# Down projections of a two-layer decoder trunk: unit by unit, in a pinned order of ScalarE and VectorE, with low parts on VectorE; two-bank attention scores; another end of the last norm

## The chip, the cores and the metric

The kernel runs on one core of a Trainium2 chip. The metric is the time of one execution in device microseconds; before the change the median of three runs is 2391.7 us (2388.97 to 2393.98). Lower is better.

## The reference

One sequence of 1024 tokens with 1024 channels passes two layers and a last RMSNorm, all in float32. Layer 0 mixes with retention heads and RWKV-7 heads, layer 1 with sliding-window attention (window 128, 16 query heads on 4 key heads, learned sinks). A SwiGLU feed-forward of width 2816 follows each. The change concerns the second product of the feed-forward, the scores of the attention and the last norm:

```python
def swiglu(h, w_gate, w_up, w_down):
    return (jax.nn.silu(h @ w_gate) * (h @ w_up)) @ w_down

s = jnp.einsum('bnqhgd,bnkhd->bnhgqk', q, kb).astype(jnp.float32) * HEAD_DIM ** -0.5   # then a band mask
h = h + mix
n = rms_norm(h, norm2_g[layer])
h = h + swiglu(n, ffn_w_gate[layer], ffn_w_up[layer], ffn_w_down[layer])
...
return rms_norm(h, final_g)
```

## The kernel before

**Layout.** Activations lie transposed: channels on the 128 partitions, tokens along the free axis, in two halves of 512 tokens. `h[0]` and `h[1]` hold the residual of the halves as 8 tiles of 128x512 each.

**Precision.** Every large product is split: an operand is rounded to the type fp32r (the high part, a ScalarE copy: `CAST` in the profile) and the rest is kept (the low part, a subtraction). A product then is three matmuls per 128x128 weight tile: high by high, high by low, low by high (`prod` L1174, `gemm` L346 to L348). A 128x512 matmul of this kind is the unit of PE's work. `vsplit` (L1345) splits weights of the down projection: high part on ScalarE (L1350), low part on GpSimd (L1351). `split` (L350) splits activations; the low part goes to GpSimd or to VectorE (L354), in the down projection half to each.

**Feed-forward.** The hidden width of 2816 is 22 tiles, taken as 11 pairs. Gate and up products follow a seven-product scheme in the manner of Strassen and Winograd: two products early (`ffn_early`) and five late (`late`, in five steps, for gate and up in lockstep with `form_down`, which prepares sums of hidden tiles for the down projection). `ffn_late` runs the eleven pairs. Hidden tiles go to the arrays `hid` in memory, their sums, split already, to `hc`.

**Down projection** (`down`, L1380). It also uses seven products in place of eight, over blocks of two output tiles, pairs of hidden tiles and the two token halves. The pairs are cut in groups: layer 0 has groups of 4 and 4 pairs (the other three pairs go through a plain product, `rest_d`), layer 1 has 4, 4 and 3. In a group there are seven stages, one per product, and in each stage four units, one for each block of output tiles (`dp`). A unit is 4 x 3 matmuls (3 x 3 in the group of three pairs) into one PSUM bank. Stage by stage:

- X, the moving operand, is either a plain hidden tile (loaded from `hid`, then split) or a prepared sum (loaded from `hc`, no split).
- Weights are loaded raw (`wdown`, 512 KB per load), combined on VectorE (`ws`, `wd`: three sums per block in the first stage, one in the third) and split before each unit.
- After a unit its bank is read: one or two VectorE adds into `h` or a helper (`vop`, L1377), or a ScalarE copy (L1411).

Four banks (tags f, f, f, y) serve stages 0 and 2, four others (m, m, r, c) stages 1, 3 and 4, the first four again stages 5 and 6 and then the next group.

**Order.** Each engine works in order. The order of the instructions on an engine is made at build time by a scheduler that follows the program's order and its own estimates of readiness; `keep` (L481) holds marked instructions in program order. SP issues nearly all DMAs. Tiles are taken from pools; a new pool on the place of a closed one waits for the last use of what lay there. PSUM has eight banks: the pool `ps` gives f three, m two, and r, c and y one each.

**Attention** (`attn`, L1498). For each of the two token halves, 4 key heads and 4 blocks of 128 queries: scores of 4 query heads (L1552, 64 rows of the array each, so e = 0 uses one half of the rows and e = 1 the other), into bank r for e = 0 and bank c for e = 1; one VectorE add of the mask per bank (L1556); maximum (L1562), exponentials, transposes, the product with V. Scores of e = 0 come first in the program, then those of e = 1.

**The last norm.** `final_r` (L1614) squares each tile on ScalarE (L1623), scales it by the gain on ScalarE (L1624), adds up squares on VectorE (L1626), sums over partitions with fp32 matmuls against a constant (L1629), and takes Ln and Exp (L1631, L1632), each with a load of its function table. For half 0 this runs beside the last two stages of the down projection; for half 1 after it. `final_out` multiplies (L1639: half 0 on GpSimd, half 1 on VectorE and GpSimd) and stores (L1640).

## Time and profile before

| | |
|---|---|
| median of three runs | 2391.7 us (2388.97, 2391.7, 2393.98) |
| profiled execution | 2394.0 us |
| its span, first to last instruction | 2392.2 us |
| mean granted clock of TensorE | 0.992 |
| down projection of layer 0 (seven products) | from 1149.5 us |
| attention, scores | 1386 to 1500 us, 1585 to 1701 us |
| down projection of layer 1 | 2151 to 2374 us |
| after its last product | 2374 to 2392 us |

Times within the execution count from the start of the span. In the views below, PE is TensorE's matmul, PEld its weight load, DVE VectorE, ACT ScalarE, POOL GpSimd and SP SyncE. A matmul's own row is longer than the distance to the next one, since they are pipelined: how much work a stretch did is read from the count of matmuls. A windows row gives the stretch, its length, then for each engine the busy time and, in brackets, the number of instructions, then the granted clock, the DMA share and GB/s. A waits row reads "who waited <- for whom: total, times, longest". A row of a line's or group's view gives minimum/median/maximum in ns, or busy us and mean ns; a timeline row gives start, duration, and in brackets the idle time before it and what ended it.

### The profile page before, as it was taken

To read this page: it belongs to the slowest core of one execution; us is meant where nothing else is said; L and a number is where in the kernel's file an instruction comes from. 1 tells how busy PE (TensorE), PEld (TensorE's weight loads), DVE (VectorE), ACT (ScalarE), POOL (GpSimd) and SP (SyncE) were. 2 spreads that over 40 slices of the span, in tenths; PEclk is the share of its full clock that TensorE was granted. 3 is DMA by queue.
4 is the path that set the end of the run, shared out by engine and by line. 5 is a ranking of instruction groups with operands and counts; after the bars stand their busy time and mean duration, and the time that the engine had idled before them with its cause. 6 is when DMAs were issued, how large, how long until landed. Compare 5 with 4: busy or idle time off the path is not lost. (4 is left out here: it accounts for less than half of the span.)

```text
span 2392.2 us, 35667 instructions
## 1 busy us (share of the span) xinstructions
PE 2318.9 (97%) x13098; PEld 1828.7 (76%) x13098; DVE 1626.3 (68%) x2462; ACT 1025.5 (43%) x1890; POOL 1193.1 (50%) x975
## 2 busy tenths in 40 slices
PE   8999899999999999999999999999999999999997
PEld 6776677777777888888778877677788788887785
DVE  5865855765567368885775469458638778887776
ACT  5354443324456333333333555455645233333336
POOL 7555331211541057776676632342232677767666
PEclk9999999999999999999999999999999999999999
DMA  7655454443445556563564321231336466547652
GB/s 267 197 204 188 154 165 133 126 128 115 146 172 181 198 171 212 195 216 137 217 222 153 118 62 58 66 131 62 106 128 220 159 217 218 203 178 274 219 200 107
DMA packets 167742, 395.93 MB, mean 166 GB/s; under 512 B 42896, under 2 KB 45584, under 8 KB 167568
## 3 DMA queue, kind: packets, MB, share of 16 engines
q1 hardware_dynamic: 164448, 388.15, 47.8%
q10 hardware_dynamic: 2832, 4.45, 0.6%
q8 instruction: 104, 1.70, 0.3%
q0 software_dynamic: 288, 1.05, 0.1%
q14 instruction: 70, 0.57, 0.1%
HBM read 271.29 MB, written 116.92 MB: 162 GB/s over the span
## 5 line engine op out<-in xcount | busy, mean ns | idle before, releaser
L332 POOL TENSOR_TENSOR w<-wr,w 128x512 fp32r<-128x512 f32 x196 | 264.3, 1354 | 427.9 <-ACT w L331 369.9
L239 PE MATMUL ps_f<-n,w 128*128 128x512 f32 x1440 | 383.5, 414 | 12.0 <-ACT w L331 6.4
L239 PEld LDWEIGHTS ps_f<-n,w 128*128 128x128 f32 x1440 | 268.3, 192 | 93.3 <-issue 21.9
L331 ACT CAST w<-wr 128x512 fp32r<-128x512 f32 x244 | 147.9, 612 | 188.8 <-PE ps_f L348 76.9
L332 POOL TENSOR_TENSOR w<-wq,w 128x512 fp32r<-128x512 f32 x92 | 130.5, 1430 | 31.7 <-ACT w L331 27.4
L346 PE MATMUL ps_f<-n,w 128*128 128x512 f32 x356 | 140.8, 396 | 2.6 <-ACT n L352 1.6
L347 PE MATMUL ps_f<-n,w 128*128 128x512 f32 x356 | 142.6, 400 | 0.0
L348 PE MATMUL ps_f<-n,w 128*128 128x512 f32 x356 | 140.1, 394 | 0.0
L1177 PE MATMUL ps_f<-n,w 128*128 128x512 f32 x322 | 127.5, 397 | 4.1 <-DVE h L1377 1.8
L1184 DVE TENSOR_TENSOR nq<-ps_m,u 128x512 f32<-128x512 f32 x88 | 58.7, 684 | 106.7 <-PE ps_m L1179 106.7
L1178 PE MATMUL ps_f<-n,w 128*128 128x512 f32 x322 | 125.5, 390 | 0.0
L1179 PE MATMUL ps_f<-n,w 128*128 128x512 f32 x322 | 125.2, 390 | 0.0
L354 POOL TENSOR_TENSOR n<-nq,n 128x512 fp32r<-128x512 f32 x64 | 106.0, 1667 | 10.2 <-ACT n L352 10.2
L1177 PE MATMUL ps_m<-n,w 128*128 128x512 f32 x282 | 110.6, 393 | 0.0
L1179 PE MATMUL ps_m<-n,w 128*128 128x512 f32 x282 | 109.8, 389 | 0.0
L1178 PE MATMUL ps_m<-n,w 128*128 128x512 f32 x282 | 109.8, 389 | 0.0
L332 POOL TENSOR_TENSOR wx<-wr,wx 128x512 fp32r<-128x512 f32 (+1 forms) x38 | 49.4, 1301 | 105.5 <-ACT wx L331 105.5
L1177 PE MATMUL ps_m<-cb,w 128*128 128x512 f32 x240 | 93.5, 389 | 0.9 <-DVE nq L1184 0.9
L1178 PE MATMUL ps_m<-cb,w 128*128 128x512 f32 x240 | 93.4, 389 | 0.0
L1179 PE MATMUL ps_m<-cb,w 128*128 128x512 f32 x240 | 93.4, 389 | 0.0
L1351 POOL TENSOR_TENSOR w<-wd,w 128x512 fp32r<-128x512 f32 (+1 forms) x53 | 75.9, 1442 | 32.0 <-ACT w L1350 31.8
L346 PEld LDWEIGHTS ps_f<-n,w 128*128 128x128 f32 x356 | 66.9, 188 | 20.0 <-ACT n L1598 2.2
(520 smaller groups left out, 6447.6 us busy)
## 6 DMA issues: line engine op xcount, KB each, us to landing
hc<-n SPq DMA_DIRECT2D x74, 512.0 KB, 2.7
wsp<-w SPq DMA_DIRECT2D x54, 512.0 KB, 3.4
w<-wsp SPq DMA_DIRECT2D x54, 512.0 KB, 3.7
wq<-in_w_gate SPq DMA_DIRECT2D x44, 512.0 KB, 4.2
u<-u SPq DMA_DIRECT2D x88, 256.0 KB, 2.9
n<-hc SPq DMA_DIRECT2D x43, 512.0 KB, 5.1
wr<-in_w_in SPq DMA_DIRECT2D x34, 512.0 KB, 5.0
hid<-n SPq DMA_DIRECT2D x66, 256.0 KB, 2.0
```

Of the source, the lines that this page charges most:

```text
L239: i = self.nc.tensor.matmul(out, lhsT, rhs, **kw)
L331: nc.scalar.copy(hi[:, :n], raw[:, c])
L332: self.lo.tensor_tensor(out=lo[:, :n], in0=raw[:, c], in1=hi.bitcast(F32)[:, :n], op=ALU.subtract)
L346: nc.tensor.matmul(ps, hi, rh, start=k == 0, stop=False)
L347: nc.tensor.matmul(ps, hi, rl, start=False, stop=False)
L348: nc.tensor.matmul(ps, lo, rh, start=False, stop=k == n - 1)
L354: e.tensor_tensor(out=lo, in0=src, in1=hi.bitcast(F32), op=ALU.subtract)
L1177: mm(ps, hi, xh, start=first and k == 0, stop=False, skip_group_check=True)
L1178: mm(ps, hi, xl, start=False, stop=False, skip_group_check=True)
L1179: mm(ps, lo, xh, start=False, stop=last and k == len(w) - 1, skip_group_check=True)
L1184: add = lambda o, x, y: V.tensor_tensor(out=o, in0=x, in1=y, op=ALU.add)
L1351: nc.gpsimd.tensor_tensor(out=lo, in0=v, in1=hi.bitcast(F32), op=ALU.subtract)
```

## The change

- `down` is written anew as a list of units. In each, in program order: the reads of the bank of the unit before (`post`); the weight split of the unit two ahead; the X split for the next stage; weight sums; loads of X two stages ahead and of the next group's weights (in stages 3 and 5); then the unit's matmuls. All ScalarE and VectorE instructions of it are chained by `pin`: each depends, for the order alone, on the one before on its engine.
- In `down` all low parts, of weights and of plain X, are on VectorE.
- For layer 0 the pool `fa` is opened, and the first weights, X and first weight split are done, before the last of the five late steps of the last feed-forward pair; a second pool `fw` (second halves of weights, sums) is opened after it. For layer 1 the first weight block is loaded into a raw tile of the feed-forward during the last pair, by one DMA more, and split there (ScalarE and GpSimd).
- Attention: the four score matmuls of a block alternate e = 0 and e = 1 and write one tile of two banks (tag rc); one VectorE add of 128x1024 takes the place of two of 128x512. The PSUM pool is closed and reopened with other tags before the attention and again before the late part of layer 1's feed-forward.
- The last norm: no scaling by the gain on ScalarE; `final_out` multiplies by gain and factor in one VectorE instruction, for both halves. Half 0's first two outputs lie in the last stage. Squares of half 1 follow each read in stages 5 and 6 of the last group (`final_after`), adds pairwise, so that two matmuls are left at the end; the table for Ln is loaded ahead.

The diff, cut to its core:

```diff
-        self.lockstep(*gens, form)
+        return zip(*gens, form)
...
-    def down(self, L, fp, fz, rest, X=()):
...
-            for dp in dps:
-                a11, a12, a21, a22 = W[dp]
-                self.prod(A[dp], self.vsplit(a11), X, True, False)
-                u0.append(self.t(fz, [P, HT], "u0", 4))
-                S.copy(u0[dp], A[dp])
-                s1.append(op(self.wsum(fp, n, 4, 8), a21, a22))
...
+    def pin(self, i):
+        k = str(i.ins.engine)
+        if k in self.pins:
+            self.tc.add_manual_dep(i.ins, self.pins[k], self.nosync, reason="order")
+        self.pins[k] = i.ins.name
+        return i
...
+        def halves(o, t, src):
+            pin(S.copy(t[0], src))
+            pin(V.tensor_tensor(out=t[1], in0=src, in1=t[0].bitcast(F32), op=ALU.subtract))
+            o.append((t[0], t[1]))
...
+        SRC = (("p", 0, 0), ("s", 2), ("p", 0, 1), ("s", 3), ("s", 4), ("s", 1), ("p", 1, 1))
+        stages = [(g, s) for g in DGROUPS[L] for s in range(7)]
...
+        for i, (si, dp) in enumerate(units):
+            gi, s = gs(si)
+            if i:
+                k = self.done(post, L, *gs(units[i - 1][0]), units[i - 1][1])
...
+            while len(ready) < 3 and i + len(ready) < len(units):
+                u, v = units[i + len(ready)]
+                if gs(u)[1] == 0 or True:
+                    ready.append(split(part(*gs(u), v)))
+            if si + 1 < len(stages):
+                prep(si + 1, dp)
+            sums(gi, s, dp)
+            if i and k is not None:
+                self.final_after(k)
+            if self.outs and s == 6 and dp > 1:
+                next(self.outs)
+            if si + 2 < len(stages):
+                get(si + 2, dp)
+            if gi + 1 < len(DGROUPS[L]):
+                if s == 3:
+                    load(gi + 1, dp)
+                if s == 5:
+                    load(gi + 1, dp + 4)
+            if gi == 0 and s == 2 and dp == 3:
+                while self.owed:
+                    self.keep(self.nc.sync.dma_start(*self.owed.pop(0)))
+                for _ in rest:
+                    pass
+            ps = banks[gi, "ABABBCC"[s]][dp]
+            self.prod(ps, ready.popleft(), XS[si], s in (0, 1, 5), s in (2, 4, 6))
...
+                ps = self.pst("rc", [P, 2, 2, 256])
+                for i in range(2):
+                    for e in range(2):
...
+                            ps[:, e, i, kw], qt[2 * g + i][a, P * b : P * b + P], src[a, P * b + P * k0 : P * b + 256],
...
-            nc.scalar.activation(h(k), h(k), AF.Copy, scale=self.col("nf", k))
...
+    def final_after(self, k):
+        sq = self.t(self.pp, [P, HT], "nq", 4)
+        self.pin(self.nc.scalar.activation(sq, self.kt(self.h[1])(k), AF.Square))
+        self.sqs.append(sq)
+        if len(self.sqs) == 3:
+            self.final_add()
...
+    def final_out(self, hf, r, order):
...
+        for k in order:
+            self.pin(
+                nc.vector.scalar_tensor_tensor(
+                    out=h(k), in0=h(k), scalar=self.col("nf", k), in1=r, op0=ALU.mult, op1=ALU.mult
+                )
+            )
             nc.sync.dma_start(self.out[k, :, hf * HT : (hf + 1) * HT], h(k))
+            yield
...
+        last = ffn_late(0, sp, K.pp, opened)[3]
+        close(gb)
         gf, fp = K.pool("fa", "left")
+        fs = [fp]
+        f = K.down(0, fs, ())
+        next(f)
+        rest(last)
+        close(gc, gs)
+        gw, fw = K.pool("fw", "left")
...
+        close(gz, gw, gf, gp)
+        gp = K.psum("pa", {"f": 3, "m": 2, "rc": 1, "y": 1})
...
+        close(gp)
+        gp = K.psum("pc", {"f": 3, "m": 2, "r": 1, "c": 1, "y": 1})
...
+        r0 = K.final_r(0, fz, order[0], 7)
+        K.keep(tc.nc.scalar.preload_act_table(AF.Ln))
+        K.outs = K.final_out(0, r0, order[0])
         run(f)
+        r1 = K.final_r1(fz)
+        run(K.outs)
+        run(K.final_out(1, r1, order[1]))
```

More of the change, by code (lines that the diff above doesn't have):

```diff
@@ new lines, in op, with split @@
+        def op(o, x, y, f=ALU.add):
+            pin(V.tensor_tensor(out=o, in0=x, in1=y, op=f))
+            return o
+        def halves(o, t, src):
+            pin(S.copy(t[0], src))
+            pin(V.tensor_tensor(out=t[1], in0=src, in1=t[0].bitcast(F32), op=ALU.subtract))
+            o.append((t[0], t[1]))
+        def split(v):
+            w, n = self.wtile(), v.shape[1]
+            t = [w[:, i, : n * P].rearrange("p (k c) -> p k c", c=P) for i in range(2)]
+            halves([], t, v)
+            return [(t[0][:, k, :], t[1][:, k, :]) for k in range(n)]
@@ new lines, in prep @@
+        def prep(si, q):
+            if q < len(raws[si]):
+                raws[si][q](XS[si])
+        load(0, 0)
+        if X:
+            XS[0] = list(X)
+        else:
+            for q in range(4):
+                get(0, q)
+            for q in range(4):
+                prep(0, q)
+        ready = deque()
+        if first is None:
+            first = split(part(0, 0, 0))
+            for i in range(1, 4):
+                load(0, i)
+            yield
+        else:
+            for i in range(1, 4):
+                load(0, i)
@@ L1452, in down @@
+        k = self.done(post, L, *gs(units[-1][0]), units[-1][1])
+        if L:
+            self.final_after(k)
         yield
@@ L1768, in trunk @@
         gf, fp = K.pool("fa", "left")
-        K.w6 = True
-        f = K.down(1, fp, fz, K.form_down(1, NP - 1, x, ts), X)
+        f = K.down(1, [fp, fp, fz], K.form_down(1, NP - 1, x, ts), X, first)
         next(f)
```

206 lines of the change are left out of this document (125 added, 81 removed).

## The prediction

> **What bounds the kernel now.** I read the page's head first, then the windows view over the two down projections and the end, then the waits of PE, then the timelines of VectorE, ScalarE and PE at the places that the windows point to.
>
> ```profile
> span 2392.2 us, 35667 instructions
> PE 2318.9 (97%) x13098; PEld 1828.7 (76%) x13098; DVE 1626.3 (68%) x2462; ACT 1025.5 (43%) x1890; POOL 1193.1 (50%) x975
> ```
>
> PE is busy 97% of the span, so the change can only win where PE stands still, where PE's own work shrinks, or behind the last product. The profiled execution took 2394.0 us, 1.8 us more than its span; it is the slowest of the three runs (median 2391.7). I sum against 2394.0 and move the result by about 1.5 us towards the median at the end.
>
> ```profile
> core 0: us, PE busy (x) PEld busy (x) DVE busy (x) ACT busy (x) POOL busy (x), PEclk, DMA share, GB/s
> 1149.50:1174.50 25.00, 21.23 (x81) 15.80 (x80) 22.94 (x21) 11.21 (x21) 18.45 (x12) 0.93 0.47 174
> 1224.50:1234.50 10.00, 8.21 (x36) 6.21 (x35) 9.93 (x11) 4.17 (x7) 6.36 (x6) 1.00 0.29 107
> 1250.00:1300.00 50.00, 50.00 (x223) 41.40 (x222) 29.71 (x34) 18.59 (x33) 37.63 (x27) 1.00 0.47 162
> 2151.00:2181.00 30.00, 27.15 (x109) 21.02 (x108) 27.74 (x28) 11.70 (x22) 21.63 (x14) 0.94 0.78 273
> 2227.00:2245.00 18.00, 13.94 (x59) 10.35 (x58) 17.93 (x19) 6.15 (x11) 11.64 (x8) 1.00 0.51 199
> 2300.00:2310.00 10.00, 9.27 (x41) 7.22 (x40) 9.94 (x16) 2.79 (x5) 4.92 (x5) 1.00 0.53 185
> ```
>
> Read the counts, not the busy time. An undisturbed stretch does 223 matmuls in 50 us, 0.224 us each. The first two rows are the first down projection: 81 and 36 matmuls are 18.2 and 8.1 us of work in 25 and 10 us, so 6.8 + 1.9 = 8.7 us are lost. The last three are the second one: 109, 59 and 41 are 24.4, 13.2 and 9.2 us, lost 5.6 + 4.8 + 0.8 = 11.2 us. Together 19.9 us, and in each of these rows VectorE is full or nearly so (9.93 of 10, 17.93 of 18). The waits of PE in these two stretches:
>
> ```profile
> PE ps_f L1178 <- POOL ha L354: 2.1, 1, 2.1
> PE ps_r L1177 <- ACT wr L1350: 1.4, 1, 1.4
> PE ps_f L1177 <- DVE h L1377: 3.1, 3, 1.6
> PE ps_f L1179 <- POOL wr L1351: 1.8, 1, 1.8
> ```
>
> Low parts on GpSimd and the adds on VectorE (L1377) that free a bank come last. Why VectorE is late:
>
> ```profile
> 1154.16 5.14 POOL L1351 TENSOR_TENSOR w<-wd,w 128x512 fp32r<-128x512 f32 x3
> ...
> 1154.67 1.78 DVE L1377 TENSOR_TENSOR ws<-wd 128x512 f32<-128x512 f32 x1
> 1165.70 0.68 DVE L1377 TENSOR_TENSOR ws<-ws,wd 128x512 f32<-128x512 f32 x1
> 1166.30 0.68 DVE L1377 TENSOR_TENSOR ws<-wd 128x512 f32<-128x512 f32 x1
> ...
> L1377 DVE TENSOR_TENSOR h<-h,ps_f x45: 672/675/689, 1184.0 to 2373.4; 128x512 f32<-128x512 f32 x45
> L1377 DVE TENSOR_TENSOR h<-h,y x40: 674/1042/1803, 1178.3 to 2349.6; 128x512 f32<-128x512 f32 x40
> ```
>
> The same kind of VectorE sum takes 1.78 us beside a GpSimd low part and 0.68 us, started every 0.60 us, while GpSimd rests. Adds with an operand in PSUM never slow down (672 to 689 ns); adds within SBUF have a median of 1042 and reach 1803 ns. So GpSimd's help costs VectorE up to 1.1 us per overlapped instruction.
>
> **The change, part by part.**
>
> *Low parts to VectorE.* A group of four pairs is 7 stages of 4 units, a unit 12 matmuls or 2.69 us, a group 28 x 2.69 = 75.3 us of PE. VectorE gets per group 28 low parts of weights, 12 of plain X, 16 weight sums and 36 adds after products: 92 instructions. At 0.68 us that is 62.6 us, 83% of 75.3. The fullest unit (second product) has two adds, a weight low part and an X low part: 4 x 0.68 = 2.7 us, just the unit; the next stages have three. The split runs two units ahead, so 5.4 us of lag are covered before PE waits; if the cover is gone, each further 0.68 us is paid. ScalarE has at most a weight cast, an X cast and one copy in a unit, under 2 us at the 0.6 us of its rows. GpSimd keeps only the four low parts of the last `form_down`, in one unit.
>
> *Order, and earlier starts.* For layer 0 the first weights, four `hid` loads, four X splits and the first weight split (five ScalarE casts, five VectorE low parts, no GpSimd) go ahead of the last step of the feed-forward. Before, PE waits 2.1 us for `ha` there. For layer 1 one more load (256 KB on SP) feeds a first split that is done before the pools open. On SP these loads pass no stores: those of the last pair are held back (`owed`) as before. The later halves of the weights still wait for freed memory; they are needed only for the sums, one unit or more later. At group changes the add that frees a bank is now pinned ahead of splits and sums. What is late next is VectorE in the third group of layer 1: units of 9 matmuls, 2.02 us, 56.5 us in all, against 44 narrow instructions and 45 full ones, plus about 15 of the final norm. Of the 19.9 us lost I leave 3.4 (a third of the start-ups, one short wait at each of three group changes, estimated from the single waits of 0.8 to 2.1 above) and take 16.5. Bounds: 19.9 if nothing waits, and below zero as in the second rival.
>
> *Clock.*
>
> ```profile
> 1165.00:1170.00 5.00, 3.46 (x11) 2.48 (x11) 5.00 (x7) 1.14 (x3) 1.79 (x2) 0.83 0.00 0
> ```
>
> The granted clock falls to 0.83 in these 5 us and is 0.94 in the 30 us at 2151, each time behind waits of about 2 us. That is inside the lost time above and goes with the waits. The Trainium skill, "TensorE: Matmul & The Clock Gate", section "Part 1: The HAM clock gate", says that the array is throttled after at least one idle window of about 3.4 us. By that rule alone no wait here is long enough, the dips would not belong to the waits and their cost (0.07 x 25 and 0.06 x 30, some 3.5 us) would stay in the sum; the trace shows a dip behind a wait of 1.4 us, so I do not follow it.
>
> *Two-bank scores.*
>
> ```profile
> 1386.00:1500.00 114.00, 21.83 (x128) 13.48 (x128) 1.00 0.19 59
> 1585.00:1701.00 116.00, 24.86 (x128) 14.41 (x128) 1.00 0.21 70
> 1450.90:1452.20 1.30, 1.14 (x8) 0.71 (x8) 1.00 0.35 57
> 1491.00:1494.00 3.00, 2.25 (x8) 1.34 (x8) 1.00 0.00 0
> ...
> L1556 DVE TENSOR_TENSOR s<-ps_r,c_amask 128x512 f32<-128x512 f32 x28 | 19.0, 680 | 10.8 <-PE ps_c L1552 10.0 <-PE ps_r L1552 0.7
> L1562 DVE TENSOR_REDUCE st<-s 128x4 f32<-128x1024 f32 x28 | 33.9, 1212 | 0.2
> ```
>
> These windows count the score matmuls (L1552) alone. A block whose two halves alternate overlaps them and takes 1.14 us; a block that the order put apart takes 2.25. All 32 blocks take 46.7 us; 28 at 1.14 and four half-sized ones would take about 34.2. Written alternately on one tile, all become ready together, so up to 12.5 us of PE time go. VectorE's two adds (2 x 0.68) become one of 1024 columns, by the reduce's row 1.21: 0.15 us x 32 = 4.8 us less. The one tile is freed later than its first half was, by half a microsecond, which the reduce that follows (1.21) covers. But the end of the first attention half is a chain, not PE:
>
> ```profile
> 1495.00:1519.00 24.00, 18.45 (x101) 11.57 (x98) 12.49 (x35) 9.76 (x31) 2.56 (x2) 0.93 0.07 23
> ```
>
> PE idles 5.5 of 24 us there, so PE time saved earlier is partly lost. I take half, 6 us; bounds 0 and 12.5.
>
> *PSUM pools.* Two more changes of pool, each between nothing and the 2.1 us of
>
> ```profile
> PE ps_m L1177 <- DVE sg L1228: 2.1, 1, 2.1
> ```
>
> which starts the second layer's late part now. I add 1 us in all; bounds 0 and 4.2.
>
> *The last norm.*
>
> ```profile
> 2374.43 0.69 DVE L1377 TENSOR_TENSOR h<-h,ps_y 128x512 f32<-128x512 f32 x1 [0.33 <-PE ps_y L1179]
> 2382.12 6.29 DVE L1639 TENSOR_TENSOR h<-h,y 128x512 f32<-128x512 f32 x5 [7.01 <-ACT y L1632]
> ...
> 2376.78 0.61 ACT L1623 ACTIVATE nq<-h 128x512 f32<-128x512 f32 x1
> 2378.17 1.28 ACT L1631 ACT_TABLE_LOAD   x1
> 2379.46 0.69 ACT L1631 ACTIVATE y<-ps_m,c_eps 128x512 f32<-128x512 f32 x1
> 2380.17 1.28 ACT L1632 ACT_TABLE_LOAD   x1
> ...
> L463 DVE SCALAR_TENSOR_TENSOR n<-h,pv,n x16: 734/776/1752, 1317.7 to 1489.7; 128x512 fp32r<-128x512 f32 x16
> ```
>
> From the last add's end (2375.1) to the factor (2382.1) are 7.0 us, with ScalarE working off squares until 2377.4. New: a square 0.6, the last matmul with its hand-overs about 1.2 (estimate), Ln 0.7, one table 1.28, Exp 0.6: 4.4, so 2.6 less. Then eight VectorE products at about 0.7 started back to back, 5.6 against 6.3 us; the six of half 0 fit in the 4.4 us before. Together 3.3 us. Against it stand those extra VectorE instructions of the third group, 0 to 6.7 us (59 x their durations against PE's time); I charge 1.3 and take 2. Bounds: 3.3 less, 3.4 more. The Trainium skill, "ScalarE: Activation LUTs", section "What ACT_TABLE_LOAD costs", puts a switch at 2.66 us with its drain; by it the preload would win 1.4 us more, but Ln starts 1.29 us after its load here, so the row decides.
>
> Sum: -16.5 - 6 + 1 - 2 = -23.5, 2394.0 - 23.5 = 2370.5, and towards the median: 2369 us.
>
> **The rivals.** *Half of it.* Waits move instead of going: PE waits for pinned VectorE work at the second product's stages and at the group changes. For it: those units are full to 2.7 of 2.69 us. Against: two units of lead. With half of the down gain and two thirds of the rest: 2394 - 10 - 4.7 = 2379, range 2378 to 2387.
>
> *Slower: VectorE's queue becomes the bound.* In a fixed order a late instruction (a sum waiting for a weight load, an add waiting for PE) stops all behind it. Price: 92 x m - 75.3 us per four-pair group, m the mean duration. It decides from m of about 0.86, where the four groups cost 4 x 3.8 and the third group of layer 1 (44 x 0.70 + 45 x 0.86 = 69.5 against 56.5) 13, some 28 us, as much as everything won. With m = 0.90 it is 4 x 7.5 + 15.6 = 46 us in place of the 19.9 now, less 7: 2413. For it: today's median is 1042 ns. Against: that is beside GpSimd, which rests then. The Trainium skill, "TensorE: Matmul & The Clock Gate", in "Engine queue depths", calls ScalarE and VectorE strict first-in-first-out; no run here contradicts it.
>
> *No change.* Other parts, ordered anew by the build, lose what these win: 2391. Nothing in the profile speaks for it, the gaps elsewhere being short.
>
> **How the numbers follow.** Forecast 0.60 (own range 2358 to 2378; the low end is 2394 - 19.9 - 12.5 - 3.3); half 0.23; no change 0.08; slower 0.09. A measurement of this kernel tells 0.2%, 4.8 us, from no change. The first two are faster: 0.83. Range 2357 to 2387 holds them less a little at the edges.
>
> **What would show it.** Right: in the down projections GpSimd near idle, VectorE near 80 to 90% with `h<-h,y` near 0.7 us, 220 or more matmuls per 50 us at every start and group change, clock 1.00; scores together below 38 us; one table load behind the last product. Wrong: PE waits on VectorE low parts in the down projections, VectorE at 98% or more across a whole group, or new waits on loads at the starts.

## The result and the profile after

The changed kernel takes 2365.86 us (median of 5 runs, 2362.65 to 2370.89) against 2391.7 (median of 5, 2388.28 to 2393.98): ratio 0.9889, 95% interval 0.9872 to 0.9906. The profiled run took 2362.65 us, the fastest of its five, as the profiled run of before (2394.0) was the slowest of its own; so the two traces lie 31.3 us apart and the medians 25.8. Head of the page:

```profile
span 2360.9 us, 35529 instructions
PE 2301.0 (97%) x13092; PEld 1818.9 (77%) x13092; DVE 1639.1 (69%) x2611; ACT 1009.7 (43%) x1872; POOL 933.6 (40%) x797
```

GpSimd's busy time fell by 260 us and VectorE's rose by 13, though VectorE has 149 instructions more. The windows that answer to those of before, at the same places of the down projections (the first three in the first layer, the last three in the second):

```profile
core 0: us, PE busy (x) PEld busy (x) DVE busy (x) ACT busy (x) POOL busy (x), PEclk, DMA share, GB/s
1152.00:1177.00 25.00, 25.00 (x112) 20.70 (x111) 19.40 (x30) 9.78 (x19) 0.00 (x0) 1.00 0.93 335
1226.50:1236.50 10.00, 10.00 (x46) 8.28 (x45) 7.11 (x12) 2.21 (x4) 0.00 (x0) 1.00 0.57 205
1250.00:1300.00 50.00, 50.00 (x222) 41.41 (x221) 37.91 (x58) 15.44 (x26) 5.16 (x4) 1.00 0.42 137
2130.20:2160.20 30.00, 30.00 (x134) 24.84 (x133) 24.52 (x40) 12.63 (x23) 0.73 (x1) 1.00 0.87 313
2206.00:2224.00 18.00, 18.00 (x81) 14.88 (x81) 14.78 (x24) 6.64 (x13) 0.00 (x0) 1.00 0.60 219
2279.00:2289.00 10.00, 10.00 (x45) 8.26 (x44) 7.50 (x14) 1.02 (x3) 0.00 (x0) 1.00 0.77 261
```

Count the matmuls: 112 in the first 25 us where 81 were, 134 in 30 us where 109 were, 81 in 18 where 59 were. VectorE does more instructions in less time (30 in 19.4 us against 21 in 22.9), and the clock column is 1.00 throughout. PE waits for nothing between 1145 and 1306 us. Its waits from 2128 us on are three:

```profile
PE ps_m L1764 <- DVE nq L1756: 3.2, 1, 3.2
PE ps_r L1181 <- DVE w L1423: 0.8, 1, 0.8
PE ps_f L1179 <- ACT w L1422: 0.7, 1, 0.7
```

The first lies behind the last product. The score matmuls alone (L1663), and the end of the first attention half:

```profile
1365.00:1695.00 330.00, 36.12 (x256) 21.56 (x256) 1.00 0.25 81
...
1483.00:1507.00 24.00, 20.05 (x114) 12.59 (x113) 17.91 (x50) 11.99 (x39) 3.92 (x3) 1.00 0.07 23
```

36.1 us where 46.7 were; and PE idles 4 of those 24 us where it idled 5.5.

Totals of this kernel wander by several us from run to run, since its first part does: the first down projection begins anywhere from 1148.9 to 1157.1 us in the runs below, with the same products in the same order before it. The stages behind that repeat better, so I count by stages, from the start of one stage's first matmul to the start of the next one's; the tail counts from 0.23 us after the start of the last product's last matmul. "Lost" is what successive matmuls of a down projection start later than 0.227 us after each other, any gap ahead of its first matmul included; 0.9 and 1.2 us of it (first and second layer) are a norm's small products and no wait. All us, from one profile each:

| kernel | first down and rest, lost | attention and early part | second down, lost | tail |
|---|---|---|---|---|
| before | 228.0, 10.2 | 468.3 | 222.8, 13.2 | 18.0 |
| after | 219.0, 0.9 | 453.2 | 214.1, 4.2 | 16.6 |
| a1 two-bank scores alone | 226.5, 8.8 | 454.8 | 221.3, 13.2 | 18.0 |
| a2 alternate order, two tiles | 226.4, 8.7 | 464.0 | 220.2, 10.7 | 18.0 |
| b2 low parts alone | 221.5, 3.8 | 469.5 | 217.0, 7.4 | 17.2 |
| b1 after, low parts on GpSimd | 219.2, 1.2 | 454.8 | 217.1, 7.1 | 16.5 |
| g1b as b1, lead of one unit | 222.2, 4.2 | 455.7 | 223.8, 13.7 | 14.7 |
| g2 after, no early starts | 224.0, 7.5 | 453.2 | 213.6, 7.4 | 14.8 |
| g2b as g2, low parts on GpSimd | 225.6, 9.2 | 454.6 | 217.2, 12.4 | 14.8 |
| b3 after, no fixed order | 219.0, 0.9 | 453.3 | 213.9, 3.9 | 19.6 |
| c1 after, GpSimd kept busy in layer 0 | 223.4, 5.3 | 453.3 | 214.1, 4.2 | 16.6 |
| d2 after, old last norm | 219.0, 0.9 | 455.8 | 214.5, 4.2 | 16.8 |
| e1 two stalls taken on | 219.0, 0.9 | 454.7 | 211.2, 1.4 | 17.0 |
| e3 as e1, three sums of squares | 219.0, 0.9 | 453.3 | 211.2, 1.4 | 15.9 |

After against before: first down projection -9.0, attention -15.1, second -8.7, tail -1.4; the late part between adds 0.8 and everything ahead of the first down projection 2.1. Sum -31.3.

Two figures of the row "before" hold a fall of TensorE's clock that other traces lack. a1 and a2 have the first down projection of before and lose 8.8 and 8.7 us in it, not 10.2: in before's trace the clock is 0.50 from 1168.27 to 1171.68 us, in theirs it is 1.00 there. And the attention stage, the same in eleven of these kernels (all but before, a2 and b2), takes 453.2 to 453.3 us in the five without such a stretch in it, 454.6 to 454.8 in the four with one of 3.41 us (a1 among them), and 455.7 to 455.8 in the two with one of 6.83. Before has one of 3.41 us there and after has none. So some 1.5 us of the -9.0 and some 1.5 us of the -15.1 are the clock's; the last section says when it falls.

### The profile page after: what moved, and what is told of

Read it like the earlier page. It is cut to its first block, busy times and chain, and to the rows that moved or that the text cites. A ratio compares the mean times of both kernels' runs of the same rounds, so it can differ in the third digit from the quotient of the medians.

```text
span 2360.9 us, 35529 instructions
## 1 busy us (share of the span) xinstructions
PE 2301.0 (97%) x13092; PEld 1818.9 (77%) x13092; DVE 1639.1 (69%) x2611; ACT 1009.7 (43%) x1872; POOL 933.6 (40%) x797
## 4 chain that ended last, share of the span: by engine, by line
PE 79%; DVE 9%; DMA 4%; ACT 3%; issue 2%; POOL 1%; SPq 1%; DVEq 0%; ACTq 0%; POOLq 0%
PE ps_f L241 8%; PE ps_m L1179 7%; PE ps_m L1181 6%; PE ps_m L1180 6%; PE ps_m L241 5%; PE ps_f L348 5%; PE ps_f L349 5%; PE ps_f L350 5%; PE ps_f L1179 4%; PE ps_f L1180 4%; PE ps_f L1181 4%; PE ps_r L1181 2%; PE ps_r L1179 2%; PE ps_r L1180 2%; PE ps_c L1181 2%
## 5 line engine op out<-in xcount | busy, mean ns | idle before, releaser
L1179 PE MATMUL ps_m<-cb,w 128*128 128x512 f32 x240 | 94.5, 394 | 4.1 <-DVE nq L1186 4.1
L333 ACT CAST w<-wq 128x512 fp32r<-128x512 f32 x92 | 55.8, 618 | 64.4 <-PE ps_m L1181 52.8
```

What stands on the lines that cost most here:

```text
L333: nc.scalar.copy(hi[:, :n], raw[:, c])
L1179: mm(ps, hi, xh, start=first and k == 0, stop=False, skip_group_check=True)
```

## The experiments

**Is attention's gain its own? (a1)** Before, with the two-bank tile, its one mask addition and the pool switches.

```diff
-                    ps = self.pst("rc"[e], [P, 2, 256])
+                ps = self.pst("rc", [P, 2, 2, 256])
+                for i in range(2):
+                    for e in range(2):
...
+        gp = K.psum("pa", {"f": 3, "m": 2, "rc": 1, "y": 1})
```

> The kernel before with the two-bank score tile, its one mask addition and the two pool switches that it needs, and nothing else of the change. Theory A (the score tile is an independent part, worth what the attention stage shows): the 32 score blocks fall from about 46.7 us to 35 or 36 us busy, the attention stage gets about 15 us shorter, the two down projections lose the same 20 us as before; total 2376 to 2380 us. Rival B (the attention stage gained because the down projection before it ended differently or because the build ordered it anew): the attention stage gains at most 5 us, total 2386 to 2392 us.

2382.08 us, ratio 0.9959 (0.9946 to 0.9972). The attention stage is 13.5 us shorter, with one stretch of half clock in it in both traces, and the down projections lose what they lost before but for the clock: theory A. The median is 2 us above the bound that I gave. The other stages did not stand still: in its trace what lies ahead of the first down projection took 5.3 us more than in that of before.

**What pairs the halves? (a2)** Before, the four matmuls of a block written alternately into its two old tiles.

```diff
-                for e in range(2):
-                    ps = self.pst("rc"[e], [P, 2, 256])
+                pse = [self.pst("rc"[e], [P, 2, 256]) for e in range(2)]
+                for i in range(2):
+                    for e in range(2):
```

> The kernel before with its four score matmuls of a block issued alternately (half 0, half 1, half 0, half 1) into the same two one-bank tiles as before, with the two mask additions kept and no pool switch. Theory A1 (the alternate order in the program is what pairs them): score blocks take about 1.14 us each, some 36 us in all, attention stage 8 to 12 us shorter, total 2379 to 2384 us. Rival A2 (the one tile is what pairs them, since with two tiles the second bank comes free one mask addition later than the first and the matmuls stand apart or all wait): score time stays above 42 us or the gain comes back as waits, attention within 4 us of before, total 2388 to 2393 us.

2386.65 us, ratio 0.9981 (0.9972 to 0.9991), 1.4 us under the rival's bound. Score matmuls alone, in the first and the second attention half:

```profile
1380.00:1500.00 120.00, 21.38 (x128) 12.83 (x128) 1.00 0.19 61
1570.00:1700.00 130.00, 24.99 (x128) 14.41 (x128) 1.00 0.25 84
```

46.4 us: nothing paired more than before, rival A2. PE's timeline shows how:

```profile
1607.45 1.13 PE L1552 MATMUL ps_r<-kc,q 64*128 64x256 f32 x4
1608.51 0.50 PE L346 MATMUL ps_f<-n,wx 128*128 128x512 f32 x1
...
1610.09 1.09 PE L1593 MATMUL ps_y<-pT,vt 128*64 128x256 f32 x8
1611.11 1.13 PE L1552 MATMUL ps_c<-ks,q 64*128 64x256 f32 x4
```

The program says r, c, r, c; the build issues the two for r (a score matmul shows as two rows), fills in six other matmuls and eight small rows, and then issues the two for c. I take it that bank c comes free later; with one tile there is one release for all four, and they stay together. The stage still got 4.3 us shorter, with the same score time; why is open.

**Low parts, order, or early starts? (b1, b2, g2, g2b)** My theory was that GpSimd is what hurt, by slowing VectorE's sums; the rival, that the order and the earlier starts win. b1 and b2 cross them:

```diff
 b1 (from after)
-            pin(V.tensor_tensor(out=t[1], in0=src, in1=t[0].bitcast(F32), op=ALU.subtract))
+            pin(self.nc.gpsimd.tensor_tensor(out=t[1], in0=src, in1=t[0].bitcast(F32), op=ALU.subtract))
 b2 (from before)
-        nc.gpsimd.tensor_tensor(out=lo, in0=v, in1=hi.bitcast(F32), op=ALU.subtract)
+        nc.vector.tensor_tensor(out=lo, in0=v, in1=hi.bitcast(F32), op=ALU.subtract)
...
-        self.split(raw, t[:, 0, :], t[:, 1, :], f % 4 < 2)
+        self.split(raw, t[:, 0, :], t[:, 1, :], L == 0 and f >= 16 and f % 4 < 2)
```

> The kernel after, with the low parts of the down projections (weights and X) back on GpSimd, in the same fixed program order, every other step of the order kept. Theory C (GpSimd is what hurt: it slows VectorE's sums within SBUF and is slow itself): VectorE adds within SBUF are back above 1 us, each low part takes 1.2 us or more, PE waits for low parts and banks return; the down projections lose 10 to 20 us more, total 2373 to 2384 us. Rival D (the fixed order, the lead of two units and the early starts are what wins; who subtracts is second): the down projections lose under 5 us more than in the kernel after, total 2363 to 2369 us.

2366.2 us, ratio 0.9895 (0.988 to 0.991): the time of the kernel after. Its first down projection, as one window, the slowest and the fullest groups on VectorE, and GpSimd's:

```profile
1148.90:1298.90 150.00, 150.00 (x662) 123.92 (x661) 89.54 (x107) 52.24 (x93) 120.07 (x83) 1.00 0.60 212
...
L1418 DVE TENSOR_TENSOR h<-h,y 128x512 f32<-128x512 f32 x16 | 14.5, 907 | 0.5
L1418 DVE TENSOR_TENSOR ws<-wd,ws 128x512 f32<-128x512 f32 x8 | 10.7, 1341 | 0.0
...
L1423 POOL TENSOR_TENSOR w<-wd,w 128x512 fp32r<-128x512 f32 x19 | 30.1, 1599 | 16.2 <-ACT w L1422 16.2
```

VectorE's sums within SBUF are nearly as slow as before (means of 0.8 to 1.3 us by group, before 0.8 to 1.4), low parts take 1.3 to 1.7 us, GpSimd is busy 80%, and PE does 662 matmuls in 150 us without a wait. My theory falls for the first layer: slow sums cost nothing there once the work runs ahead. In the second layer GpSimd costs 3.0 us (217.1 against 214.1). Most of that lies in one place, where PE waits for loads of `hc` (1.6 us in all) and for casts, and every other engine is idle most of the time:

```profile
2180.00:2200.00 20.00, 16.98 (x70) 12.47 (x69) 6.96 (x10) 5.41 (x10) 8.23 (x7) 1.00 0.83 307
```

The low parts of the last feed-forward pair, which go out to `hc` and come back, stand on GpSimd's queue there; that this is what makes the loads late was not tried.

> The kernel before with the low parts of its down projections on VectorE, with no fixed order, no early start and no block order. Theory C (GpSimd is what hurt): VectorE sums go back to about 0.7 us and most of the 20 us lost in the down projections go, total 2374 to 2381 us. Rival D (the order is what wins; VectorE with 92 instructions a group and no order makes late the additions that free banks): the down projections lose as much as before or more, total 2388 to 2400 us.

2384.68 us, ratio 0.9971 (0.996 to 0.9982), above the bounds of C and below those of D. Without any of the order the two down projections lose 3.8 + 7.4 us instead of 10.2 + 13.2: two thirds of what the whole change wins there. All of PE's waits in them:

```profile
PE ps_f L1178 <- DVE ha L354: 2.1, 1, 2.1
PE ps_f L1179 <- DVE wr L1351: 3.7, 1, 3.7
...
2148.00:2158.00 10.00, 6.23 (x19) 4.53 (x20) 9.60 (x16) 2.57 (x6) 0.87 (x1) 0.83 0.92 348
2158.00:2340.00 182.00, 182.00 (x805) 150.75 (x804) 145.51 (x241) 71.51 (x126) 5.62 (x4) 1.00 0.63 221
```

One wait in each layer, at its start; then 805 matmuls in 182 us with none. So low parts on VectorE cure the middle, and the starts stay. Next, the early starts taken out:

```diff
-        next(f)
         rest(last)
         close(gc, gs)
+        next(f)
...
-            first = K.vsplit(raw, True) if L else None
+            first = None
```

In this kernel and the next one, half 0's norm factor is taken ahead of the second down projection and leaves out what that projection adds, which also moves work into that stage and out of the tail. So their total times are not those of the full function, and I read their first layer alone.

> The kernel after without the earlier starts: the first layer's first weights, loads and splits stand behind the feed-forward's last step, and the second layer's first weight split behind the change of pools; low parts on VectorE, units, lead and fixed order stay. Theory S (the earlier starts cure the waits at the beginning of each down projection and nothing else): a wait of 2 to 3 us at the first layer's first product and of 2 to 4 us at the second's come back, nothing later in either; first down projection with the rest 221 to 222 us instead of 219.0, second 216.5 to 218.5 instead of 214.05; total 2369 to 2373 us. Rival (lead and order hide the late start): both within 1 us of the kernel after, total 2364 to 2368 us.

2372.88 us, ratio 0.9916 (0.9901 to 0.993). PE's waits and two windows of the first layer:

```profile
PE ps_f L1181 <- DVE wr L1423: 1.9, 1, 1.9
PE ps_f L1179 <- ACT wr L1422: 1.7, 1, 1.7
...
1151.00:1161.00 10.00, 6.41 (x17) 4.31 (x16) 7.50 (x12) 3.43 (x8) 0.00 (x0) 0.67 0.88 338
1161.00:1301.00 140.00, 140.00 (x618) 115.92 (x617) 108.49 (x167) 47.51 (x84) 2.94 (x2) 1.00 0.52 186
```

All 6.6 us more than in the kernel after (7.5 against 0.9) lie in these first 10 us: theory S in kind, dearer than the 2 to 3 I expected, since there are two waits and the clock is 0.50 from 1154.48 to 1161.31, from the second wait on (0.67 over the window).

> As the run before this one, with the low parts on GpSimd besides: what is left of the change in the down projections is the program order by units, the lead of two units and the fixed order. Theory S (starts by starting early, the middle by low parts on VectorE or by lead and order): the waits at the starts are back (GpSimd's, 3 to 6 us in each layer), the middle of the first layer stays without waits; first down projection 222 to 225 us, second 219 to 222 us, total 2374 to 2380 us. Rival (order and lead alone do it all): 219 to 220.5 and 214 to 217.5 us, total 2364 to 2369 us. Rival (they do nothing without the early start): 226 to 228 and 221 to 223 us, as in the kernel before.

2380.6 us, ratio 0.9952 (0.9938 to 0.9965). The same view, with GpSimd at work:

```profile
PE ps_f L1181 <- POOL wr L1423: 4.3, 1, 4.3
...
1165.00:1305.00 140.00, 140.00 (x617) 115.56 (x616) 83.84 (x97) 50.03 (x89) 113.28 (x77) 1.00 0.56 193
```

The start costs 4.3 us and the same 1.7 as in g2; behind it 617 matmuls stand in 140 us although GpSimd is busy for 113 of them. So the units with their lead, too, cure the middle. In the first layer the three cures give, in us lost:

| kernel | lost |
|---|---|
| none (before, a1, a2) | 8.7 to 10.2 |
| units alone (g2b) | 9.2 |
| units, low parts on VectorE (g2) | 7.5 |
| low parts on VectorE alone (b2) | 3.8 |
| units, early starts (b1) | 1.2 |
| all (after) | 0.9 |

The middle had two cures, each enough in this layer; in the second, VectorE's saves 3 us more. The start is less simple: b2, without early starts, waits 2.1 us there, and g2, which adds the units, loses 3.7 us more than b2, some 2 of them by the half clock. The list of units takes the four X splits ahead of the first weight split, so PE waits for a weight cast that starts behind four X casts:

```profile
1152.56 0.61 ACT L1422 CAST wr<-wd 128x512 fp32r<-128x512 f32 x1
```

In b2 that cast starts at 1150.71, ahead of them. So the units by themselves make the start dearer, and the early start pays for that too. The early start in the order of before was not tried.

**Is the lead what covers GpSimd? (g1b)** As b1, one unit of lead in place of two.

```diff
-            while len(ready) < 3 and i + len(ready) < len(units):
+            while len(ready) < 2 and i + len(ready) < len(units):
```

> The kernel with the low parts back on GpSimd in the fixed order (early starts kept), with the weight splits running one unit ahead instead of two. Theory L (the lead is what hides GpSimd's 1.3 to 1.6 us per low part; a unit with a weight and an X low part needs 2.9 of 2.69 us): waits for GpSimd's low parts appear in the middle of both layers; first down projection 222 to 232 us instead of 219.2, second 219 to 230 instead of 217.1; total 2372 to 2390 us. Rival (one unit is enough, the lead is not what counts): within 1.5 us of the run with two units, total 2364 to 2369 us.

2372.41 us, ratio 0.992 (0.9907 to 0.9934): 3.0 us more than b1 in the first layer and 6.7 in the second, the first at the low end and the second in the middle of what I expected. The second layer's waits of PE:

```profile
PE ps_f L1179 <- DMA ha<-hc: 2.2, 2, 2.0
PE ps_f L1179 <- ACT w L1422: 2.0, 2, 1.6
PE ps_f L1181 <- POOL w L1423: 1.8, 3, 1.0
```

Casts and low parts come late now, and the same loads as in b1. So the second unit of lead covers part of GpSimd's slowness, as theory L has it.

**Does the fixed order matter? (b3)** After, with `pin` returning its instruction unchanged.

```diff
-        k = str(i.ins.engine)
-        if k in self.pins:
-            self.tc.add_manual_dep(i.ins, self.pins[k], self.nosync, reason="order")
-        self.pins[k] = i.ins.name
         return i
```

> The kernel after without the fixed order: the same instructions on the same engines, written in the same program order, but each engine's order in the down projections is left to the build. Theory P (the fixed order is what keeps the additions that free banks ahead of splits and sums): the first down projection and the rest up to the second half's start lose 4 to 8 us more than the 219.0 us of the kernel after, the second 3 to 6 us more than 214.0; total 2372 to 2380 us. Rival Q (what counts is the program order by units, the lead and the earlier starts; the pins only write down what the build does anyway): both within 2 us of the kernel after, total 2363 to 2369 us.

2367.18 us, ratio 0.9893 (0.9873 to 0.9912). Both down projections keep their lengths (219.0, and 213.9 against 214.1): rival Q. The tail alone differs, 3.0 us longer. VectorE's timeline there, and the two sums of squares:

```profile
2338.82 5.39 DVE L1771 SCALAR_TENSOR_TENSOR h<-h,pv,y 128x512 f32<-128x512 f32 x8 [1.52 <-ACT y L1739]
2344.12 0.68 DVE L1414 TENSOR_TENSOR h<-h,ps_f 128x512 f32<-128x512 f32 x1
...
2349.20:2353.10 3.90, 3.78 (x4) 1.17 (x4) 0.01 (x1) 0.02 (x1) 0.00 (x0) 0.50 0.01 2
```

The build lets all eight products of half 0 go as soon as their factor is there, and the last additions stand 5.4 us behind them; PE then rests 4.5 us, and its sums take 3.78 us at half clock against 1.98 at 1.00 in the kernel after. So 1.8 of the 3.0 us are the clock's, and 1.2 remain for the order.

**Does GpSimd beside a full VectorE cost time? (c1)** After, and in the first layer GpSimd makes one more subtraction per weight split into a tile that nothing reads; its operand is the weight tile.

```diff
+            junk = self.t(fs[2], [P, HT], "jk", 1)[:, : n * P].rearrange("p (k c) -> p k c", c=P)
+            self.nc.gpsimd.tensor_tensor(out=junk, in0=t[0].bitcast(F32), in1=t[0].bitcast(F32), op=ALU.subtract)
```

> The kernel after, and in the first layer's down projection alone GpSimd does one further subtraction of 128x512 (for narrow weights less) after each weight split, into a tile that nothing reads, so that nobody waits for it; the second layer is the control. Theory C (GpSimd beside VectorE slows VectorE's operations within SBUF): VectorE's sums and low parts there go from 0.68 us to a mean of 0.9 to 1.2 us; additions from PSUM stay at 0.68. For PE, theory C1 (the prediction's price: 92 instructions a group times the mean duration against 75.3 us): with a mean over all of 0.85 to 0.95 us the two groups lose 6 to 24 us; total 2370 to 2390 us. Rival C2 (two units of lead and GpSimd pausing part of each unit cover it): the stage stays within 3 us of 219.0 us, total 2363 to 2369 us. Control: the second layer's down projection stays at 214 us.

2371.34 us, ratio 0.9908 (0.9894 to 0.9923). The first down projection in one window, three of VectorE's groups, and two of ScalarE's waits:

```profile
1157.10:1307.10 150.00, 147.40 (x644) 120.01 (x644) 141.80 (x175) 48.83 (x85) 72.61 (x57) 1.00 0.56 197
...
L1423 DVE TENSOR_TENSOR w<-ws,w 128x512 fp32r<-128x512 f32 x15 | 17.0, 1135 | 0.0
L1418 DVE TENSOR_TENSOR h<-h,y 128x512 f32<-128x512 f32 x16 | 14.0, 874 | 0.5
L1418 DVE TENSOR_TENSOR h<-h,ps_f 128x512 f32<-128x512 f32 x15 | 10.1, 676 | 2.2 <-PE ps_f L1181 2.2
...
ACT w L1422 <- POOL jk L1433: 10.6, 5, 3.7
ACT wr L1422 <- POOL jk L1433: 9.2, 5, 2.3
```

Work whose result nobody reads slows VectorE's instructions within SBUF to 0.87 and 1.14 us and leaves those from PSUM at 0.68. VectorE is busy 94.5%, and the stage is 4.4 us longer, between C1 and C2; the control, the second layer, stands at 214.1. So the slowing is shown. That it alone costs the 4.4 us is not: the subtraction reads the weight tile, so ScalarE's casts into the next use of that tile wait for it ten times, 19.8 us in all (last two lines), and never in the kernel after. VectorE waits for such casts only 2.4 us, which speaks for the slowing as the larger part. In b1 VectorE had room: GpSimd did the low parts, and VectorE was busy 89.5 of 150 us.

**What is the new last norm worth? (d2)** After, with the norm of before.

```diff
-        r1 = K.final_r1(fz)
-        run(K.outs)
-        run(K.final_out(1, r1, order[1]))
+        r1 = K.final_r(1, fz, order[1], 4)
+        K.final_out(0, r0, order[0], "pppppppp")
+        K.final_out(1, r1, order[1], "vpvvpvvp")
```

> The kernel after with the last norm of the kernel before (eight squares and weighted copies of half 1 late on ScalarE, two table loads behind the last product, products shared by VectorE and GpSimd). Theory N (the new norm saves about 2 us net): from the last product's end to the span's end 17.5 to 18.5 us instead of 16.6, and VectorE has less to do in the third group of the second layer, which changes PE's losses there by less than 1 us; total 1 to 2 us above the kernel after, 2365 to 2370 us. Rival (the norm's extra VectorE work in the third group costs as much as it saves): the second down projection gets 1.5 us shorter or more, total as the kernel after or below.

2364.49 us, ratio 0.9885 (0.9867 to 0.9903): tail 16.8 us against 16.6, second down projection 0.4 longer. The new norm is worth 0.6 us by the stages and nothing that the times can tell. Most of the tail's 1.4 us came with the rest of the change, since d2 has the old norm and 1.2 of them; by which part of it was not tried.

**Two stalls taken on (e1, e3).** In e1 half 0's products leave the last stage and the table load takes their place; the last feed-forward subtractions and their low parts are spread over units, on VectorE.

```diff
-            if self.outs and s == 6 and dp > 1:
-                next(self.outs)
+            if self.outs and s == 6 and dp == 2:
+                self.pin(self.nc.scalar.preload_act_table(AF.Ln))
...
+            if gi == 0 and s in (3, 4) and dp % 2 and L:
+                next(rest, None)
```

> The kernel after with two of its remaining stalls taken on. First, no products of half 0's output are placed inside the last stage, and the last table load before the factor is placed in that stage: the last addition should start about 0.7 us after the last product instead of 1.9, and the tail fall from 16.6 to 14 to 15.5 us; rival: half 0's products then stand behind the factor and take what is won, tail 16 to 17.5 us. Second, the last feed-forward pair's subtractions and splits are spread over units of the third and fourth products, on VectorE instead of GpSimd: the wait of 0.8 us at 2169 goes and no VectorE operation there takes over 1 us; second down projection 213 to 213.6 us instead of 214.05; rival: the wait moves to the place where the four tiles are used. Total 1.5 to 3.5 us below the kernel after, 2361 to 2365 us.

2361.95 us, ratio 0.9873 (0.9852 to 0.9893). The second down projection gains 2.9 us, more than expected: both waits of the kernel after go, the one at 2169 and the one for ScalarE at 2339, whose casts stood behind three table loads. The last addition starts at 2343.97, 0.3 us behind the last product instead of 1.9. Yet the tail is 17.0 us. PE behind the last product:

```profile
2345.64 3.67 PE L1769 MATMUL ps_m<-nq,c_ones 128*128 128x512 f32 x4 [2.01 <-DVE nq L1761]
```

The two sums of squares take 3.67 us at a mean granted clock of 0.55 (rows in the last section); in the kernel after they took 1.98 at 1.00. Without these 1.7 us the tail would be 15.3, as expected; so it is the clock, and not the rival's products of half 0, that takes the gain back. e3 tries to keep PE at work there, with three sums instead of two, the first of which needs less:

```diff
-        if len(self.sqs) == 3:
+        if len(self.sqs) == 4:
...
-            nc.tensor.matmul(ps, self.cst["ones"], sq, start=i == 0, stop=i == 1)
+            nc.tensor.matmul(ps, self.cst["ones"], sq, start=i == 0, stop=i == 2)
```

> The kernel with the two stalls taken on (last additions first, feed-forward splits spread), and the sum of squares of half 1 given to TensorE as three products (six squares summed, the seventh, the eighth) instead of two, so that the first of them starts right behind the last product of the down projection. Theory T (TensorE's 2.0 us of rest there and the half clock behind it, 3.7 us for two such products, are on the path): the products end 2 to 2.6 us earlier, the factor is ready at about the time when VectorE has done half 0's eight products, tail 14.5 to 15.5 us instead of 17.0; total 2359 to 2362 us. Rival (VectorE's eight products of half 0 then stand in front of half 1's): tail 16 us or more.

2360.12 us (2355.5 to 2363.63), ratio 0.9867 (0.985 to 0.9884), the lowest of all; its interval overlaps that of the kernel after, so that it is the better one rests on its stages (second down projection -2.9 us, tail -0.7). The tail, 15.9, lies between the two expectations:

```profile
2345.19 2.84 PE L1769 MATMUL ps_m<-nq,c_ones 128*128 128x512 f32 x6 [1.68 <-DVE nq L1761]
```

PE rests for 1.68 us all the same, as VectorE's addition that the first sum needs stands behind the last additions to `h`. The three sums take 2.84 us at the full clock, 0.86 more than two would; e3 is ahead of e1 because its clock did not fall. The last section shows how much of that is where the ticks of its clock lay, so it is one execution's luck in part. Theory T's idea, to start early, was not reached.

## Why the prediction was right, and where its steps were not

The forecast was 2369 us, the result is 2365.9, and faster was the likeliest. The gain lies in the places that I named; the size of the attention's part, and half of the reason given for the down projections, I had wrong.

*Down projections, -16.5.* Measured -17.7. I left 3.4 us lost; 4.2 + 0.9 remain, of which 2.1 are norm products and 3.0 waits and what follows them. Some 1.5 us of the gain are the clock's, as said. The signs hold: 222 matmuls in 50 us, GpSimd without an instruction in most windows, clock 1.00, VectorE at 71 to 82% (a little under the 80 to 90 I gave), `h<-h,y` within SBUF back from a median of 1042 ns to a mean of

```profile
L1418 DVE TENSOR_TENSOR h<-h,y 128x512 f32<-128x512 f32 x16 | 11.1, 692 | 0.5
```

*The reason for it.* I wrote that GpSimd's help costs VectorE up to 1.1 us per overlapped instruction and put the waits down to that. The slowing is as I read it, but as the cause of PE's waits it is half the story. Moving the low parts alone (b2) wins 12.2 of the 23.4 us lost; but in b1 the slowing is all there, and PE loses nothing to it in the first layer. There two units of lead cure the middle without moving anything off GpSimd, and early starts cure the start. The step that failed is the one from "VectorE is full in each of these rows" to "therefore its speed is the cause": it was full of sums that could have been done earlier.

*Places left.* I expected a third of the start-ups and a wait at each group change. Start-ups and group changes have none; what stays is where the kernel still uses GpSimd (VectorE at 1.78 us at 2166 us) and where ScalarE loads tables.

*The slower rival's price, 92 x m - 75.3.* The m of that sum is a mean duration, but VectorE's rows overlap: durations of 0.68 us start every 0.60. In c1 the mean duration is 0.87 us, so the price is 4.6 us a group and 9 for the two groups. By busy time an instruction takes 141.80 / 175 = 0.81 us, so the price is nothing. The stage lost 4.4, between the two, and part of that may be ScalarE's waits. So the price by durations is too dear here, and where its edge lies stays open. In the kernel after the mean duration is 0.70, and there is room.

*Pinning.* I counted on it to keep the additions that free banks ahead of splits; in b3 the program order by units does so by itself.

*Two-bank scores, -6.* Measured -13.5 alone (a1) and -15.1 in the change, of which 1.5 are the clock's: the term that I mis-sized most, and above my bound of 12.5. The score matmuls gave 10.6 of the 12.5 us allowed, and none of it was lost again in the chain at the end of the half, which itself became shorter (PE idle 4 of 24 us, before 5.5). Where the other 2.9 us come from was not taken apart. Taking half because that end is not PE's was wrong: the saved time lies ahead of the chain, and the chain starts earlier by it.

*Pool switches, +1.* The late part is 0.8 us longer. *Last norm, -2.* -1.4 in the tail, of it only 0.2 by the new norm (d2). The working was off in two places, both in VectorE's and PE's rows of the kernel after:

```profile
2345.68 0.74 DVE L1775 SCALAR_TENSOR_TENSOR h<-h,pv,y 128x512 f32<-128x512 f32 x1
2346.34 0.68 DVE L1418 TENSOR_TENSOR h<-h,ps_y 128x512 f32<-128x512 f32 x1
...
2347.68 1.98 PE L1764 MATMUL ps_m<-nq,c_ones 128*128 128x512 f32 x4 [3.25 <-DVE nq L1756]
```

The last addition starts at 2346.34, 1.9 us behind the last product's end, as pinned products of half 0 stand ahead of it; and the sum of squares that I estimated at 1.2 us takes 1.98.

*The clock.* The dips went with the waits and came back with them in b2, g2 and e1, as I took it. The Trainium skill, "TensorE: Matmul & The Clock Gate", "Part 1: The HAM clock gate", has the array throttled after at least one idle window of about 3.4 us. In g2 the 3.41 us ahead of the fall at 1154.48 hold one wait, of 1.7 us, and PE is busy in them for 1.46 us; the measurement decides. The length agrees, since the clock's steps here are 3.41 us long; that TensorE must be idle for all of it does not. That a dip follows every such wait does not hold either, see the last section.

That the forecast came within 3 us is luck in part, since two errors met: attention gave 9 us more than forecast, while the medians lie 5.5 us closer together than the two profiled runs.

## What to carry to other kernels

When an engine is full ahead of a wait, ask first whether its work could have begun earlier: an early start and a lead of two units took away all the waits of the first layer here and some half of the loss in the second, with the slow helper left in place. Matmuls that should run as a pair belong in one tile: with two tiles this build parted most of them. And where totals wander by several us, compare the lengths of single stages: the first down projection agrees to 0.01 us in the five kernels that share it without a change (after, b3, d2, e1, e3). Where a stage repeats less well, look for a stretch of half clock in it first.

## What was not expected of the hardware

A GpSimd subtraction slows VectorE within SBUF and not from PSUM, even when nothing reads its result (c1: 874 to 1135 ns against 676).

How long TensorE rested does not say by itself whether its clock falls; where the rest lies counts too. Cut into steps of 3.41 us, the ends of e1, the kernel after and e3 read:

```profile
2342.25:2345.66 3.41, 1.40 (x8) 0.82 (x6) 3.17 (x7) 3.06 (x4) 0.00 (x0) 1.00 0.00 0
2345.66:2349.07 3.41, 3.41 (x4) 1.15 (x4) 3.41 (x6) 0.00 (x0) 0.00 (x0) 0.50 0.58 216
...
2342.95:2346.36 3.41, 1.48 (x7) 0.90 (x5) 3.41 (x7) 1.26 (x2) 0.00 (x0) 1.00 0.20 77
2346.36:2349.77 3.41, 1.98 (x4) 0.68 (x4) 3.41 (x7) 0.70 (x2) 0.00 (x0) 1.00 0.39 146
...
2343.09:2346.50 3.41, 1.73 (x5) 0.68 (x5) 3.41 (x7) 2.16 (x3) 0.00 (x0) 1.00 0.00 0
2346.50:2349.90 3.40, 1.53 (x4) 0.38 (x2) 3.40 (x6) 1.81 (x2) 0.00 (x0) 1.00 0.97 360
```

In the fourteen traces of this case the granted clock is 1.00 or 0.50 and nothing between; a figure such as 0.83 is a mean over a window. Of the dips, 105 end within the span, and each lasts 3.41 or 6.83 us. All dips of a trace start on ticks that lie whole steps of 3.41 us apart, at other places in each execution. What the step ahead of a tick holds goes with what follows: of the steps at full clock (from 10 us on), all 53 in which PE was busy less than 40% were followed by a dip, and 1 of 9271 in which it was busy more than 66%. In between it goes either way, 65 dips behind 204 steps; PE's ends are modelled, so the shares are rough. A rest of 3.25 us in the kernel after lies across a tick (2346.36) and leaves the step ahead of it busy for 1.48 us, and the clock stays; a rest of 2.0 us in e1 lies within one step, with 1.40 us busy, and costs 1.7 us. All three lie near the edge, and the ticks lie elsewhere in each execution, so I would not expect another execution of the same kernel to end the same way.

Score matmuls on 64 rows overlap in pairs whether their outputs share a tile or not. In a2, with two tiles, a block that the build had left together (the one at 1404.6 us) took 1.14 us, as long as one of before did.
